# Rotating q and k out of PSUM, with the norm's factor moved behind the rotation

## The chip, the core and the metric

The kernel runs on one core of one Trainium2 chip. Its time is the device time of one execution in microseconds (us). A core has five engines that run beside each other, each through its own queue in order: TensorE (PE; its weight loads are listed as PEld), VectorE (DVE), ScalarE (ACT), GpSimd (POOL) and SyncE (SP), which here issues the loads. They wait for one another through semaphores. Matrix products land in PSUM, which has eight banks; all other tiles are in SBUF.

## What is computed

One layer of a hybrid encoder, 256 positions of width 2048, in float32. The input projection of the normalised x gives q, k, v and two halves of a gated convolution. q and k are normalised per head vector of 128, rotated and used in differential attention: four heads with two softmaxes each, of which the second is subtracted with a factor. The output projection and a gated feed-forward layer follow. The part around the change:

```python
xn = rms_norm(h, norm1_g[l])
proj = jnp.einsum('bsd,dn->bsn', xn, w_in[l].astype(xn.dtype))
...
q = apply_rope(rms_norm(q, q_norm_g[l]), cos, sin)
k = apply_rope(rms_norm(k, k_norm_g[l]), cos, sin)
...
s = jnp.einsum('bqhcd,bkhcd->bhcqk', q_blk, k).astype(jnp.float32) * scale
s = jnp.where(mask[None, None, None], s, -jnp.inf)
p = jax.nn.softmax(s, axis=-1)
w = p[:, :, 0] - lam * p[:, :, 1]
return jnp.einsum('bhqk,bkhe->bqhe', w.astype(v.dtype), v)
...
att = rms_norm(att, subln_g[l]) * (1.0 - lambda_init)
```

The rotation is linear, so a factor per position and head vector may be applied before it or behind it; for q it may also be applied to the scores.

## The kernel before

Every large product is made of reduced-precision passes: an operand is split into a rounded part `hi` and a rest `lo`, and three matmuls (hi by hi, lo by hi, hi by lo) take the place of one. The weights stream through in **chunks** of 256 rows by 512 columns. For each chunk SyncE loads `raw`, ScalarE casts it to `whi` (`round_chunk`, L324), VectorE subtracts to `wlo` (`split_chunk`, L333), and TensorE multiplies (`multiply`): a first half of eight matmuls with `whi` (L363, L364) and a second half of four with `wlo` (L369), for the two row halves m = 0 and 1 of the sequence, into two PSUM banks `acc`. `whi` and `wlo` have three buffers each, and both are queued two chunks ahead.

`run_chunks` walks the chunks in one order: four column blocks for the convolution, then blocks k, q, k, q, v, v (eight chunks each, the very first block nine), then the output projection and the feed-forward layer. Counted from 0, the first q block ends with chunk 48, the second k block with 56, the second q block with 64, the v blocks with 72 and 80.

All other work is written as generators that are started when a block is done. `resume` steps each of them once in the middle of a chunk's multiplication and once at its end, so a `yield` is half a chunk and `lag(n)` is n of them. What a generator queues at a step stands in its engine's queue at that place and is executed in that order. Between these steps `run_side` puts the taps of the convolution (L549, `y`) on VectorE as long as a credit of time lasts, from which other work is deducted by `spend`. `room(n, hold)` holds a generator back until n of the four auxiliary PSUM banks are free by the program's own count `held`.

The steps around the change: `qk_rows`, for a block of q or k and one m, squares the four head vectors out of PSUM (`square_sum`, L459, ScalarE), makes the factor `f` on GpSimd (`rsqrt_mean` and L647; the power is L222), scales into `qn` (L651, ScalarE), rotates (L658 to L661, VectorE), transposes (L666, TensorE) and copies into `qT` or `kT` (L667, ScalarE). `attend_scores`, for a head, makes the scores `ps_s` (L682), masks them, takes the maximum `nmx` (L692), the exponentials `pr` (L701), the combined weights `wt` (L712 to L715) and their transposes (L723 to L725). `attend_values` multiplies with v into `ps_o` (L749), squares that (L459), makes the factor `ro` on GpSimd, scales to `att` (L763), transposes to `ps_at` (L771) and splits into `mahi` and `malo` (or `ahi` and `alo`; `split_scaled`, L237 and L238).

Of the kernel before, what the change touches and what calls it, by code (L numbers as in the profile page):

```python
# [18 lines left out]
P = 128  # L19
# [44 lines left out]
RAW_BUFS = 5  # L64
AUX = 4

LAG = (3, 2, 6)
HL_BUFS = 3

KTILE_US = 1.30  # L70
# [56 lines left out]
def tile_block(  # L127
# [143 lines left out]
    def spend(us):  # L271
        credit[0] -= us
# [181 lines left out]
    xT = {}  # L454
    rstd1 = [const.tile([P, 1], F32, tag=f"rstd1_{m}", name=f"rstd1_{m}") for m in range(NM)]

    def square_sum(src, accum, **kw):
        junk = pre.tile([P, N], F32, tag="junk", name="junk", bufs=1)
        act.activation(junk[:, : src.shape[-1]], src, AF.Square, accum_out=accum, **kw)  # L459
# [178 lines left out]
    def qk_rows(key, b, m, ps):  # L638

        G = N // DH  # L640
        spend(1.65)
        ss = small.tile([P, G], F32, tag="ssq", name="ssq")
        for j in range(G):
            square_sum(ps[:, j * DH : (j + 1) * DH], ss[:, j : j + 1], scale=rstd1[m])
        f = small.tile([P, G], F32, tag="fq", name="fq")
        rsqrt_mean(f, ss, DH, EPS)
        pool.tensor_scalar(f, f, rstd1[m], 0.0, ALU.mult, ALU.add)  # L647
        yield from lag(LAG[0])
        qn = pre.tile([P, G, DH], F32, tag="va", name="qn")
        for j in range(G):  # L650
            act.activation(qn[:, j, :], ps[:, j * DH : (j + 1) * DH], AF.Copy, scale=f[:, j : j + 1])  # L651
# [4 lines left out]
        hd = DH // 2  # L656
        bc = lambda ap, n: ap.unsqueeze(1).to_broadcast([P, G, n])
        dve.tensor_tensor(t1, qn, bc(tab[:, 0, :], DH), ALU.mult)  # L658
        dve.tensor_tensor(t2[:, :, :hd], qn[:, :, hd:], bc(tab[:, 1, :hd], hd), ALU.mult)
        dve.tensor_tensor(t2[:, :, hd:], qn[:, :, :hd], bc(tab[:, 1, hd:], hd), ALU.mult)  # L660
        dve.tensor_tensor(t1, t1, t2, ALU.add)  # L661
# [8 lines left out]
    wTs = {}  # L670
    eps_s = small.tile([P, H, NM], F32, tag="eps_s", name="eps_s", bufs=1)

    def attend_scores(hd):
        scs = []
        yield
        yield from room(2, 2)
        for m in range(NM):
            L = (m + 1) * P
            sc = aux_ps.tile([P, 2, S], F32, tag="aux", name="ps_s")
            for c in range(2):  # L680
                g = 2 * hd + c
                pe.matmul(sc[:, c, :L], qkT["q"][:, g, m * P : (m + 1) * P], qkT["k"][:, g, :L],  # L682
                          start=True, stop=True)
            scs.append(sc)
        yield from lag(2)
        nmxs, prs, sms = [], [], []
        for m in range(NM):
            L = (m + 1) * P
            sc = scs[m]
            dve.memset(sc[:CHUNK, :, L - CHUNK : L], MASKED)  # L690
            nmx = small.tile([P, 2], F32, tag="nmx", name="nmx")
            dve.tensor_reduce(nmx, sc[:, :, :L], AX.X, ALU.max, negate=True)  # L692
            nmxs.append(nmx)
        spend(0.1)
        yield from lag(3)
        for m in range(NM):
            L = (m + 1) * P
            pr = pre.tile([P, 2, S], F32, tag="pr", name="pr", bufs=4)
            sm = small.tile([P, 2], F32, tag="sm", name="sm")
            for c in range(2):  # L700
                act.activation(pr[:, c, :L], scs[m][:, c, :L], AF.Exp, bias=nmxs[m][:, c : c + 1],  # L701
                               accum_out=sm[:, c : c + 1])
            prs.append(pr)
            sms.append(sm)
        held[0] -= 2
        yield from lag(2)
        wts = []
        for m in range(NM):
            L = (m + 1) * P
            r = small.tile([P, 1], F32, tag="r", name="r")  # L710
            c = small.tile([P, 1], F32, tag="a1", name="c")
            dve.reciprocal(r, sms[m][:, 1:2])  # L712
            dve.scalar_tensor_tensor(c, sms[m][:, 0:1], neg_lam, r, ALU.mult, ALU.mult)
            wt = pre.tile([P, S], F32, tag="wt", name="wt", bufs=4)
            dve.scalar_tensor_tensor(wt[:, :L], prs[m][:, 1, :L], c, prs[m][:, 0, :L], ALU.mult, ALU.add)  # L715
            pool.tensor_scalar(eps_s[:, hd, m : m + 1], sms[m][:, 0:1], sms[m][:, 0:1], E * EPS, ALU.mult, ALU.mult)
# [6 lines left out]
        pe.transpose(pt[:, 0, :], wts[0][:, :P], ident)  # L723
        pe.transpose(pt[:, 1, :], wts[1][:, :P], ident)
        pe.transpose(pt[:, 2, :], wts[1][:, P:], ident)  # L725
# [14 lines left out]
    def attend_values(hd):  # L740
        while hd not in wTs:
            yield
        wT = wTs.pop(hd)
        atts = []
        yield from room(1, 1)
        o = aux_ps.tile([P, NM, E], F32, tag="aux", name="ps_o")
        for m in range(NM):
            for k in range(m + 1):
                pe.matmul(o[:, m, :], wT[:, (0 if m == 0 else 1 + k), :], v_sb[k][:, hd * E : (hd + 1) * E],  # L749
                          start=k == 0, stop=k == m)  # L750
        yield
        ss = small.tile([P, NM], F32, tag="sso", name="sso")
        for m in range(NM):
            square_sum(o[:, m, :], ss[:, m : m + 1])
        r = small.tile([P, NM], F32, tag="ro", name="ro")
        t = small.tile([P, 8], F32, tag="rsq", name="rsq")
        pool.tensor_tensor(ss, ss, eps_s[:, hd, :], ALU.add)
        pool.tensor_scalar(t[:, :NM], ss, 1.0 / E, 0.0, ALU.mult, ALU.add)
        pool.tensor_tensor(r, t[:, :NM], neghalf[:, :NM], ALU.pow)
        yield from lag(2)  # L760
        for m in range(NM):
            at_ = pre.tile([P, E], F32, tag="att", name="att", bufs=4)
            act.activation(at_, o[:, m, :], AF.Copy, scale=r[:, m : m + 1])  # L763
            atts.append(at_)
        held[0] -= 1
        yield
        yield from room(1)
        pt = aux_ps.tile([P, 2, S], F32, tag="aux", name="ps_at")
        for e in range(2):
            for m in range(NM):  # L770
                pe.transpose(pt[:, e, m * P : (m + 1) * P], atts[m][:, e * P : (e + 1) * P], ident)  # L771
# [526 lines left out]
```

## Time and profile before

| | |
|---|---|
| runs | 1041.3 us median of 3 (1040.77 to 1041.76) |
| profiled execution | 1042.43 us, span 1040.7 us |
| granted TensorE clock | 1.0 in every slice |
| q, k and v blocks with the attention | about 95 to 250 us of the span |

A row of a timeline has the start in us from the span's start, the time taken, engine, line and operation, the tile written and those read, sizes and count, and in brackets the engine's idle time before it with what ended that. A row of a group has count, busy us, the mean ns of one, and the idle time before. Matmuls overlap, so their progress is read from start to start.

### The profile page before, as it was taken

To read this page: it belongs to the slowest core of one execution; us is meant where nothing else is said; L and a number is where in the kernel's file an instruction comes from. 1 tells how busy PE (TensorE), PEld (TensorE's weight loads), DVE (VectorE), ACT (ScalarE), POOL (GpSimd) and SP (SyncE) were. 2 spreads that over 40 slices of the span, in tenths; PEclk is the share of its full clock that TensorE was granted. 3 is DMA by queue.
4 is the path that set the end of the run, shared out by engine and by line. 5 is a ranking of instruction groups with operands and counts; after the bars stand their busy time and mean duration, and the time that the engine had idled before them with its cause. 6 is when DMAs were issued, how large, how long until landed. Compare 5 with 4: busy or idle time off the path is not lost.

```text
span 1040.7 us, 13006 instructions
## 1 busy us (share of the span) xinstructions
PE 1028.6 (99%) x4639; PEld 847.4 (81%) x4639; DVE 925.5 (89%) x1117; ACT 642.2 (62%) x796; POOL 115.4 (11%) x159
## 2 busy tenths in 40 slices
PE   8999999999999999999999999999999999999998
PEld 7888887877888788888888888888888888888786
DVE  7899889899775599999999898989999989889887
ACT  7554666656656565776665656666757556667452
POOL 0130123222000100000102011000001110000010
PEclk9999999999999999999999999999999999999999
DMA  9657644554546667987989899879798979797773
GB/s 336 225 182 277 221 165 150 174 167 137 180 152 230 187 236 242 275 258 223 264 238 261 286 234 278 258 238 265 222 272 246 282 217 294 232 259 230 215 222 101
DMA packets 115664, 237.59 MB, mean 228 GB/s; under 512 B 7696, under 2 KB 8848, under 8 KB 115344
## 3 DMA queue, kind: packets, MB, share of 16 engines
q1 hardware_dynamic: 104864, 203.71, 58.2%
q0 software_dynamic: 10592, 33.04, 16.4%
q8 instruction: 36, 0.59, 0.2%
q14 instruction: 28, 0.23, 0.1%
q10 hardware_dynamic: 144, 0.03, 0.0%
HBM read 204.24 MB, written 9.44 MB: 205 GB/s over the span
## 4 chain that ended last, share of the span: by engine, by line
PE 62%; DVE 1%; DMA 1%; issue 0%; ACT 0%; DVEq 0%
PE q L1058 11%; PE q L1052 11%; PE q L1053 11%; PE q L1033 9%; PE q L1031 9%; PE q L1032 9%; PE acc L369 1%; DMA wlo<-raw 1%; PE ps_a L856 1%; PE acc L364 1%; PE acc L363 1%; DVE wlo L333 0%; DVE wlt L1014 0%; DVE wt L1004 0%; ACT wh L1010 0%
## 5 line engine op out<-in xcount | busy, mean ns | idle before, releaser
L324 ACT CAST whi<-raw 128x1024 fp32r<-128x1024 f32 (+1 forms) x257 | 265.8, 1049 | 119.7 <-PE acc L364 60.1
L333 DVE TENSOR_TENSOR wlo<-raw,whi 128x1024 fp32r<-128x1024 f32 (+1 forms) x211 | 253.8, 1215 | 43.0 <-ACT whi L324 42.7
L1010 ACT CAST wh<-wt 128x2048 fp32r<-128x2048 f32 x60 | 114.9, 1915 | 109.2 <-DVE wt L1006 109.1
L1014 DVE TENSOR_TENSOR wlt<-wt,wh 128x2048 fp32r<-128x2048 f32 x60 | 137.4, 2290 | 19.5 <-ACT wh L1010 19.4
L363 PE MATMUL acc<-whi,xhi 128*128 128x512 f32 x320 | 126.4, 395 | 2.4 <-ACT whi L324 2.3
L1052 PE MATMUL q<-whi,chi 128*128 128x512 f32 x320 | 125.2, 391 | 0.0
L364 PE MATMUL acc<-whi,xlo 128*128 128x512 f32 x320 | 124.8, 390 | 0.0
L1053 PE MATMUL q<-whi,clo 128*128 128x512 f32 x320 | 124.6, 389 | 0.0
L1031 PE MATMUL q<-wh,fhi 128*128 128x512 f32 x280 | 109.8, 392 | 0.0
L1032 PE MATMUL q<-wh,flo 128*128 128x512 f32 x280 | 108.9, 389 | 0.0
L1013 DVE TENSOR_TENSOR wlb<-wb,wh 128x1536 fp32r<-128x1536 f32 x60 | 105.1, 1751 | 1.0 <-ACT wh L1007 1.0
L549 DVE SCALAR_TENSOR_TENSOR y<-upad,cw,y 128x256 f32<-128x256 f32 x240 | 101.9, 479 | 2.2 <-ACT y L542 2.2
L328 POOL DMA_DIRECT2D wlo<-raw x46 | 39.7, 863 | 507.6 <-ACT wlo L327 294.3
L369 PE MATMUL acc<-wlo,xhi 128*128 128x512 f32 x320 | 87.8, 396 | 2.0 <-DVE wlo L333 1.9
L1007 ACT CAST wh<-wb 128x1536 fp32r<-128x1536 f32 x60 | 88.5, 1474 | 0.4 <-DMA wb<-in_w_gate_dram 0.4
L1058 PE MATMUL q<-wlo,chi 128*128 128x512 f32 x320 | 85.7, 390 | 0.6 <-DMA wlo<-raw 0.6
L1052 PE MATMUL q<-whi,ahi 128*128 128x512 f32 x192 | 74.9, 390 | 0.0
L1053 PE MATMUL q<-whi,alo 128*128 128x512 f32 x192 | 74.7, 389 | 0.0
L1004 DVE TENSOR_TENSOR wt<-wb 128x1024 f32<-128x1024 f32 x60 | 73.0, 1217 | 0.0
L363 PEld LDWEIGHTS acc<-whi,xhi 128*128 128x128 f32 x320 | 60.1, 188 | 15.6 <-ACT whi L324 3.3
L369 PEld LDWEIGHTS acc<-wlo,xhi 128*128 128x128 f32 x320 | 59.3, 188 | 15.5 <-DVE wlo L333 3.6
L1058 PEld LDWEIGHTS q<-wlo,chi 128*128 128x128 f32 x320 | 59.9, 188 | 13.7 <-DMA wlo<-raw 1.2
(244 smaller groups left out, 1844.4 us busy)
## 6 DMA issues: line engine op xcount, KB each, us to landing
raw<-in_w_in_dram SPq DMA_DIRECT2D x79, 512.0 KB, 4.7
raw<-in_w_gate_dram SPq DMA_DIRECT2D x48, 512.0 KB, 5.4
raw<-in_w_up_dram SPq DMA_DIRECT2D x48, 512.0 KB, 5.2
raw<-in_w_down_dram SPq DMA_DIRECT2D x48, 512.0 KB, 7.1
wlo<-raw POOLq DMA_DIRECT2D x46, 512.0 KB, 7.3
wb<-in_w_up_dram SPq DMA_DIRECT2D x40, 512.0 KB, 4.5
wb<-in_w_gate_dram SPq DMA_DIRECT2D x40, 512.0 KB, 5.9
wb<-in_w_down_dram SPq DMA_DIRECT2D x40, 512.0 KB, 6.1
```

The costliest lines, as they stand in the source:

```text
L324: act.copy(c["hi"], c["raw"])
L333: dve.tensor_tensor(c["lo"], c["raw"], c["hi"].bitcast(F32), ALU.subtract)
L363: pe.matmul(ps[m], xhi[:, ms], hi[:, j, :], start=c["first"] and j == 0, stop=False)
L364: pe.matmul(ps[m], xlo[:, ms], hi[:, j, :], start=False, stop=False)
L369: pe.matmul(ps[m], xhi[:, ms], lo[:, j, :], start=False, stop=c["last"] and j == nk - 1)
L1010: act.copy(c["hi"][:, :SUMMED], c["t"])
L1014: dve.tensor_tensor(lot, c["t"], c["hi"][:, :SUMMED].bitcast(F32), ALU.subtract)
L1031: pe.matmul(ps, hi, c["hi"][:, w], start=bool(first), stop=False)
L1032: pe.matmul(ps, lo, c["hi"][:, w], start=False, stop=False)
L1052: pe.matmul(ps, xs[i][0][:, ms], hi[:, i, :], start=i == 0 and bool(c["first"].get(qs[m])), stop=False)
L1053: pe.matmul(ps, xs[i][1][:, ms], hi[:, i, :], start=False, stop=False)
L1058: pe.matmul(sum_bank(c, qs[m]), xs[i][0][:, ms], lo[:, i, :], start=False, stop=i == 1 and bool(c["last"].get(qs[m])))
```

## The change

`qk_rows` no longer makes `qn`. The squares are taken without the first norm's factor; the epsilon term that this factor brings in is made once for each m (`eps1`). The rotation reads the projection out of PSUM, with no factor. k's factor is applied by ScalarE behind the rotation, in place; q's factor goes into the exponential as its `scale`, and the maximum `nmx` is multiplied with it. The lags are shorter, and the copies out of the transposes are queued `COPY_LAG` half chunks later, with the PSUM bank held as long. In `attend_values` both halves are first rounded by ScalarE and then split by VectorE, and one GpSimd step is folded into the squares' scale.

```diff
-MASKED = -3.0e38
+MASKED = -1.0e30
...
-LAG = (3, 2, 6)
+LAG = (1, 3, 3)
+COPY_LAG = 2
...
+            pool.tensor_scalar(eps1[m], ss[:, m : m + 1], -2.0 * EPS / D, EPS * EPS, ALU.mult, ALU.add)
...
         for j in range(G):
-            square_sum(ps[:, j * DH : (j + 1) * DH], ss[:, j : j + 1], scale=rstd1[m])
-        f = small.tile([P, G], F32, tag="fq", name="fq")
-        rsqrt_mean(f, ss, DH, EPS)
-        pool.tensor_scalar(f, f, rstd1[m], 0.0, ALU.mult, ALU.add)
+            square_sum(ps[:, j * DH : (j + 1) * DH], ss[:, j : j + 1], scale=DH ** -0.5)
+        f = small.tile([P, G], F32, tag="f" + key, name="f" + key, bufs=4)
+        pool.tensor_scalar(ss, ss, eps1[m], 1.0, ALU.add, ALU.mult)
+        pool.tensor_tensor(f, ss, neghalf[:, :G], ALU.pow)
+        if key == "q":
+            fqs[b, m] = f
         yield from lag(LAG[0])
-        qn = pre.tile([P, G, DH], F32, tag="va", name="qn")
-        for j in range(G):
-            act.activation(qn[:, j, :], ps[:, j * DH : (j + 1) * DH], AF.Copy, scale=f[:, j : j + 1])
-        yield from lag(LAG[1])
...
-        dve.tensor_tensor(t1, qn, bc(tab[:, 0, :], DH), ALU.mult)
-        dve.tensor_tensor(t2[:, :, :hd], qn[:, :, hd:], bc(tab[:, 1, :hd], hd), ALU.mult)
-        dve.tensor_tensor(t2[:, :, hd:], qn[:, :, :hd], bc(tab[:, 1, hd:], hd), ALU.mult)
+        dve.tensor_tensor(t1, raw, bc(tab[:, 0, :], DH), ALU.mult)
+        dve.tensor_tensor(t2[:, :, :hd], raw[:, :, hd:], bc(tab[:, 1, :hd], hd), ALU.mult)
+        dve.tensor_tensor(t2[:, :, hd:], raw[:, :, :hd], bc(tab[:, 1, hd:], hd), ALU.mult)
         dve.tensor_tensor(t1, t1, t2, ALU.add)
-        yield from lag(LAG[2])
-        yield from room(1)
+        yield from lag(LAG[1])
+        if key == "k":
+            for j in range(G):
+                act.activation(t1[:, j, :], t1[:, j, :], AF.Copy, scale=f[:, j : j + 1])
+            yield from lag(LAG[2])
+        yield from room(1, 1)
         pt = aux_ps.tile([P, G, P], F32, tag="aux", name="ps_qk")
         for j in range(G):
             pe.transpose(pt[:, j, :], t1[:, j, :], ident)
+        yield from lag(COPY_LAG)
+        held[0] -= 1
         act.copy(qkT[key][:, b * G : (b + 1) * G, m * P : (m + 1) * P], pt)
...
+            f = fqs[hd // 2, m][:, hd % 2 * 2 : hd % 2 * 2 + 2]
+            dve.tensor_tensor(nmx, nmx, f, ALU.mult)
...
                 act.activation(pr[:, c, :L], scs[m][:, c, :L], AF.Exp, bias=nmxs[m][:, c : c + 1],
-                               accum_out=sm[:, c : c + 1])
+                               scale=fs[m][:, c : c + 1], accum_out=sm[:, c : c + 1])
...
-            split_scaled(mixa[2 * hd + e], pt[:, e, :], col("sg", e))
+            act.activation(mixa[2 * hd + e][0], pt[:, e, :], AF.Copy, scale=col("sg", e))
+        for e in range(2):
+            hi, lo = mixa[2 * hd + e]
+            dve.scalar_tensor_tensor(lo, pt[:, e, :], col("sg", e), hi.bitcast(F32), ALU.mult, ALU.subtract)
```

The instructions move. VectorE's queue at the first q block, before (`wlo` are those of chunks 52, 53 and 54; `t` is the rotated tile, `y` the taps of the convolution):

```order
L549 SCALAR_TENSOR_TENSOR y<-upad_127,cw,y 128x256 x2
L333 TENSOR_TENSOR wlo<-raw,whi 128x1024 x3
L658 TENSOR_TENSOR t_1515<-qn,gcsq_588 128x512
L659 TENSOR_TENSOR t_1516<-qn,gcsq_588 128x4x64
L660 TENSOR_TENSOR t_1516<-qn,gcsq_588 128x4x64
L661 TENSOR_TENSOR t_1515<-t_1515,t_1516 128x512
L549 SCALAR_TENSOR_TENSOR y<-upad_127,cw,y 128x256 x3
L333 TENSOR_TENSOR wlo<-raw,whi 128x1024
```

And with the change, at the same place, where the lines from L324 on are numbered one higher and the rotation is L661 to L664:

```order
L553 SCALAR_TENSOR_TENSOR y<-upad_129,cw,y 128x256 x2
L334 TENSOR_TENSOR wlo<-raw,whi 128x1024
L661 TENSOR_TENSOR t_1456<-acc,gcsq_592 128x512
L662 TENSOR_TENSOR t_1457<-acc,gcsq_592 128x4x64
L663 TENSOR_TENSOR t_1457<-acc,gcsq_592 128x4x64
L664 TENSOR_TENSOR t_1456<-t_1456,t_1457 128x512
L334 TENSOR_TENSOR wlo<-raw,whi 128x1024
L661 TENSOR_TENSOR t_1492<-acc,gcsq_596 128x512
L662 TENSOR_TENSOR t_1493<-acc,gcsq_596 128x4x64
L663 TENSOR_TENSOR t_1493<-acc,gcsq_596 128x4x64
L664 TENSOR_TENSOR t_1492<-t_1492,t_1493 128x512
L334 TENSOR_TENSOR wlo<-raw,whi 128x1024
```

The two rotations of a block stand two chunks earlier, one behind the `wlo` of chunk 52 and one behind that of 53, and read `acc`, the PSUM bank. TensorE's transposes of the rotated q move with them, from the ends of chunks 55 and 56 to the middles of 52 and 53.

ScalarE's queue behind the v copies, where head 0's output is squared (`junk,sso`), before; `att` is head 0's, then head 1's, and `pr` the exponentials of head 2, the only ones there:

```order
L734 ACTIVATE v_134<-acc,rstd_1_123 128x512
L324 CAST whi<-raw 128x1024 x2
L459 ACTIVATE junk,sso<-ps_o 128x256 x4
L324 CAST whi<-raw 128x1024
L763 ACTIVATE att<-ps_o,ro 128x256 x2
L701 ACTIVATE pr,sm<-ps_s,nmx 128x128 x2
L701 ACTIVATE pr,sm<-ps_s,nmx 128x256 x2
L237 ACTIVATE mahi<-ps_at,cols 128x256 x2
L763 ACTIVATE att<-ps_o,ro 128x256 x2
```

With the change, at the same place (`pr` is first head 2's, then head 3's):

```order
L747 ACTIVATE v_136<-acc,rstd_1_123 128x512
L325 CAST whi<-raw 128x1024
L714 ACTIVATE pr,sm<-ps_s,nmx,fq 128x128 x2
L714 ACTIVATE pr,sm<-ps_s,nmx,fq 128x256 x2
L325 CAST whi<-raw 128x1024
L462 ACTIVATE junk,sso<-ps_o 128x256 x4
L325 CAST whi<-raw 128x1024
L714 ACTIVATE pr,sm<-ps_s,nmx,fq 128x128 x2
L714 ACTIVATE pr,sm<-ps_s,nmx,fq 128x256 x2
L774 ACTIVATE att<-ps_o,ro 128x256 x2
L786 ACTIVATE mahi<-ps_at,cols 128x256 x2
L774 ACTIVATE att<-ps_o,ro 128x256 x2
```

The exponentials of head 3 have come up from behind head 1's split to a place ahead of head 0's `att`.

More of the change, by code (lines that the diff above doesn't have):

```diff
@@ L455, in tile_block @@
     rstd1 = [const.tile([P, 1], F32, tag=f"rstd1_{m}", name=f"rstd1_{m}") for m in range(NM)]
+    eps1 = [const.tile([P, 1], F32, tag=f"eps1_{m}", name=f"eps1_{m}") for m in range(NM)]
     def square_sum(src, accum, **kw):
@@ L656, in qk_rows @@
         hd = DH // 2
+        raw = ps.rearrange("p (g d) -> p g d", g=G)
         bc = lambda ap, n: ap.unsqueeze(1).to_broadcast([P, G, n])
-        dve.tensor_tensor(t1, qn, bc(tab[:, 0, :], DH), ALU.mult)
-        dve.tensor_tensor(t2[:, :, :hd], qn[:, :, hd:], bc(tab[:, 1, :hd], hd), ALU.mult)
-        dve.tensor_tensor(t2[:, :, hd:], qn[:, :, :hd], bc(tab[:, 1, hd:], hd), ALU.mult)
+        dve.tensor_tensor(t1, raw, bc(tab[:, 0, :], DH), ALU.mult)
+        dve.tensor_tensor(t2[:, :, :hd], raw[:, :, hd:], bc(tab[:, 1, :hd], hd), ALU.mult)
+        dve.tensor_tensor(t2[:, :, hd:], raw[:, :, :hd], bc(tab[:, 1, hd:], hd), ALU.mult)
         dve.tensor_tensor(t1, t1, t2, ALU.add)
-        yield from lag(LAG[2])
-        yield from room(1)
+        yield from lag(LAG[1])
[4 more added lines that the diff above has]
+        yield from room(1, 1)
         pt = aux_ps.tile([P, G, P], F32, tag="aux", name="ps_qk")
@@ L670, in tile_block @@
     wTs = {}
+    fqs = {}
     eps_s = small.tile([P, H, NM], F32, tag="eps_s", name="eps_s", bufs=1)
@@ L685, in attend_scores @@
         yield from lag(2)
-        nmxs, prs, sms = [], [], []
+        nmxs, fs, prs, sms = [], [], [], []
         for m in range(NM):
@@ L692, in attend_scores @@
             dve.tensor_reduce(nmx, sc[:, :, :L], AX.X, ALU.max, negate=True)
+            f = fqs[hd // 2, m][:, hd % 2 * 2 : hd % 2 * 2 + 2]
+            dve.tensor_tensor(nmx, nmx, f, ALU.mult)
             nmxs.append(nmx)
+            fs.append(f)
         spend(0.1)
@@ L753, in attend_values @@
         for m in range(NM):
-            square_sum(o[:, m, :], ss[:, m : m + 1])
+            square_sum(o[:, m, :], ss[:, m : m + 1], scale=E ** -0.5)
         r = small.tile([P, NM], F32, tag="ro", name="ro")
-        t = small.tile([P, 8], F32, tag="rsq", name="rsq")
         pool.tensor_tensor(ss, ss, eps_s[:, hd, :], ALU.add)
-        pool.tensor_scalar(t[:, :NM], ss, 1.0 / E, 0.0, ALU.mult, ALU.add)
-        pool.tensor_tensor(r, t[:, :NM], neghalf[:, :NM], ALU.pow)
+        pool.tensor_tensor(r, ss, neghalf[:, :NM], ALU.pow)
         yield from lag(2)
```

2 lines of the change are left out of this document (1 added, 1 removed).

## The prediction

> **What bounds the kernel now.** I read the page's busy times first: TensorE is busy for nearly the whole span.
>
> ```profile
> PE 1028.6 (99%) x4639; PEld 847.4 (81%) x4639; DVE 925.5 (89%) x1117; ACT 642.2 (62%) x796; POOL 115.4 (11%) x159
> ```
>
> So an edit on the other engines is worth only the time in which TensorE stands still. Then the windows, here two of 25 us in the stage of the change (the span, then busy time and count of PE, PEld, DVE, ACT and POOL): TensorE misses 0.80 and 1.14 us in them.
>
> ```profile
> 150.00:175.00 25.00, 24.20 (x113) 19.77 (x113) 21.55 (x38) 16.61 (x40) 6.66 (x10) 1.00 0.43 138
> 200.00:225.00 25.00, 23.86 (x113) 19.57 (x111) 22.65 (x41) 13.96 (x28) 4.83 (x5) 1.00 0.49 161
> ```
>
> TensorE's timeline shows each place. Starts follow each other every 0.23 us (163.42 to 163.65); what a start comes later than that is lost.
>
> ```profile
> 163.42 0.39 PE L363 MATMUL acc<-whi,xhi 128*128 128x512 f32 x1
> 163.65 0.39 PE L364 MATMUL acc<-whi,xlo 128*128 128x512 f32 x1
> 164.83 1.21 PE L369 MATMUL acc<-wlo,xhi 128*128 128x512 f32 x4 [0.80 <-DVE wlo L333]
> 190.50 0.39 PE L364 MATMUL acc<-whi,xlo 128*128 128x512 f32 x1
> 190.98 0.73 PE L369 MATMUL acc<-wlo,xhi 128*128 128x512 f32 x2
> 213.99 0.39 PE L364 MATMUL acc<-whi,xlo 128*128 128x512 f32 x1
> 215.52 0.97 PE L369 MATMUL acc<-wlo,xhi 128*128 128x512 f32 x3 [1.14 <-DVE wlo L333]
> 250.05 0.39 PE L364 MATMUL acc<-whi,malo 128*128 128x512 f32 x1
> 250.55 0.30 PE L723 MATMUL ps_wt<-ident,wt 128*128 128x128 f32 x1
> 251.31 0.33 PE L724 MATMUL ps_wt<-ident,wt 128*128 128x128 f32 x1 [0.46 <-DVE wt L715]
> 251.47 0.27 PE L725 MATMUL ps_wt<-ident,wt 128*128 128x128 f32 x1
> 262.67 0.39 PE L364 MATMUL acc<-whi,malo 128*128 128x512 f32 x1
> 263.43 0.67 PE L771 MATMUL ps_at<-ident,att 128*128 128x128 f32 x4 [0.37 <-DVE alo L238]
> ```
>
> Three times a second half waits for `wlo`: 1.18 - 0.23 = 0.95, 0.48 - 0.23 = 0.25 and 1.53 - 0.23 = 1.30 us, together **2.50**. The weights of head 3 come late: 0.50 - 0.23 = 0.27, and 0.76 less the 0.16 from one transpose to the next, 0.60, together **0.87**. The last transposes of `att` come late by 0.76 - 0.23 = **0.53**. In all 3.90 us, the most that better order can give here.
>
> Why is `wlo` late? VectorE's, ScalarE's and GpSimd's timelines around the first q block:
>
> ```profile
> 148.78 2.35 DVE L333 TENSOR_TENSOR wlo<-raw,whi 128x1024 fp32r<-128x1024 f32 x2
> 154.51 1.22 DVE L333 TENSOR_TENSOR wlo<-raw,whi 128x1024 fp32r<-128x1024 f32 x1 [3.38 <-ACT whi L324]
> 155.65 0.69 DVE L658 TENSOR_TENSOR t<-qn,gcsq 128x512 f32<-128x512 f32 x1
> 157.04 0.69 DVE L661 TENSOR_TENSOR t<-t,t 128x512 f32<-128x512 f32 x1
> 157.65 1.27 DVE L549 SCALAR_TENSOR_TENSOR y<-upad,cw,y 128x256 f32<-128x256 f32 x3
> 148.59 3.40 POOL L222 TENSOR_TENSOR fq<-rsq,neghalf 128x4 f32<-128x4 f32 x1
> 147.80 0.19 ACT L459 ACTIVATION_READ_ACCUMULATOR junk<-acc,rstd 128x1 f32 x1
> 150.58 0.19 ACT L459 ACTIVATION_READ_ACCUMULATOR junk<-acc,rstd 128x1 f32 x1
> 152.40 1.14 ACT L651 ACTIVATE qn<-acc,fq 128x128 f32<-128x128 f32 x4 [1.62 <-POOL fq L647]
> 153.41 1.07 ACT L324 CAST whi<-raw 128x1024 fp32r<-128x1024 f32 x1
> 205.60 1.23 DVE L333 TENSOR_TENSOR wlo<-raw,whi 128x1024 fp32r<-128x1024 f32 x1 [2.28 <-ACT whi L324]
> ```
>
> ScalarE stands before `qn` until GpSimd's power is done; the cast `whi` is queued behind that, and VectorE idles 3.38 us for it. Then VectorE has two rotations to make up and falls behind. At the second q block it idles 2.28 us in the same way, before the wait at 215.52.
>
> **The change part by part.** *The scaling between squares and rotation goes.* ScalarE loses 32 `qn` (four take 1.14 us above, so 9 us) and has 16 of the same form behind k's rotation, off the path both. VectorE's rotation keeps its time if a read of PSUM costs what a read of SBUF does.
>
> ```profile
> L788 DVE TENSOR_TENSOR h<-h,acc 128x512 f32<-128x512 f32 x8 | 5.1, 680 | 0.0
> L713 DVE SCALAR_TENSOR_TENSOR c<-sm,neg_lam,r 128x1 f32<-128x1 f32 x8 | 1.8, 220 | 0.4
> ```
>
> An add of that size with one operand in PSUM takes 680 ns, the rotation's own, wholly in SBUF, 0.69 us (157.04): I take no difference. [...]
>
> Now walk VectorE's queue in its new order (its rows stand in the section on the change) from where it stood, 148.78, though it should be earlier, since k's copies no longer hold ScalarE. One `wlo` is 1.13 to the next start (half of 148.78's pair), a rotation 157.65 - 155.65 = 2.00. First rotation 149.91 to 151.91: the squares that it must follow ended at 147.99. `wlo`, then second rotation 153.04 to 155.04; its squares ended at 150.77. Third `wlo` from 155.04, done 1.22 later at 156.26. TensorE's second halves stood there:
>
> ```profile
> 152.53 1.07 PE L369 MATMUL acc<-wlo,xhi 128*128 128x512 f32 x4
> 157.97 1.07 PE L369 MATMUL acc<-wlo,xhi 128*128 128x512 f32 x4
> ```
>
> The one at 157.97 takes that `wlo`, so it is 1.7 us early, and VectorE never idles. The 0.95 goes; the second q block has the same pattern (2.28 idle), so the 1.30 goes. The 0.25 lies in the k block, where softmax and rotation came on one another's heels; they stand apart now. All 2.50 is taken as gained. On the other side of that bound stands zero, if `wlo` is late for another reason.
>
> *Added on VectorE:* eight tiny products on `nmx`, by the nearest row 0.22 us each, 1.8 us over some 60 us; the windows show VectorE idle over 2 us in each 25. Nothing on the path, and 0.2 us each if that cover were gone. *Exponentials with a second pointer operand:* ScalarE's rows with none, one and two pointers (L459, L763, L611) differ by 87 and 88 ns.
>
> ```profile
> L459 ACT ACTIVATE junk<-ps_o 128x256 f32<-128x256 f32 x8 | 3.1, 385 | 7.9 <-PE ps_o L749 7.7
> L763 ACT ACTIVATE att<-ps_o,ro 128x256 f32<-128x256 f32 x8 | 3.3, 472 | 0.0
> L611 ACT ACTIVATE z<-ps_ln,cols 128x256 f32<-128x256 f32 x8 | 4.2, 560 | 1.2 <-DVE mclo L615 1.1
> ```
>
> *Transposes and scores move two or three chunks ahead*; TensorE does the same number, so nothing for itself. *Copies queued later* end ScalarE's waits for transposes, which were beside the path. *The two halves of the split of `att`* no longer take turns: `att` of head 3 is some 0.6 us earlier, which covers the 0.53. Head 3's weights are transposed in the middle of chunk 79 in place of 82; VectorE makes them right behind that chunk's `wlo`, and no longer runs behind there, so I take the 0.87 as gained. If VectorE is as late there as at 250.55, it stays.
>
> *A new wait.* Head 3's four exponentials now stand ahead of head 0's `att` (ScalarE's rows in the section on the change). Before:
>
> ```profile
> 231.94 0.60 PE L771 MATMUL ps_at<-ident,att 128*128 128x128 f32 x4
> 230.33 0.84 ACT L763 ACTIVATE att<-ps_o,ro 128x256 f32<-128x256 f32 x2
> 231.06 0.37 ACT L701 ACTIVATE pr<-ps_s,nmx 128x128 f32<-128x128 f32 x1
> 232.64 0.51 ACT L237 ACTIVATE mahi<-ps_at,cols 128x256 fp32r<-128x256 f32 x1
> 262.67 0.83 ACT L763 ACTIVATE att<-ps_o,ro 128x256 f32<-128x256 f32 x2
> ```
>
> ScalarE's place there is tied to TensorE (it squares `ps_o` as soon as that is made), so it doesn't come earlier. The exponentials take 232.64 - 231.06 = 1.58, with the second pointer 1.58 + 4 x 0.09 = 1.94. `att` starts at 230.33 + 1.94 = 232.27, and from its start to the transposes are 263.43 - 262.67 = 0.76: 233.03, against 231.94. New loss **1.1 us**; 0.7 if the pointer hides in the overlap, none if the order leaves ScalarE ahead. Behind it wait `mahi`, head 1's `att` and its transposes, half a chunk later.
>
> Sum: 3.90 - 1.1 = **2.8 us** gained. The profiled execution took 1042.43 (span 1040.7), so 1039.6; that execution was 1.1 above the median of the runs, 1041.3, and so I forecast 1038.5.
>
> **The rivals.** *No new wait* at head 0: 3.9 gained, 1037.4. For it: exponentials may be done before the squares are. Against: they are queued behind them.
>
> *TensorE reaches the rotated q too early.* The transposes now follow the rotation by 1.5 chunks. In the walk the first rotation's last row ends at 149.91 + 1.39 + 0.69 = 151.99, TensorE arrives at 152.53: only 0.54 early. Where VectorE is 0.9 later than walked, each q block loses some 0.5: 1.0 off the gain, 1039.5. [...]
>
> *The waits stay*, because `wlo` is late by VectorE's load and not by its idling: 0.87 + 0.53 - 1.1 = 0.3 gained, 1041.0. Against it: the 3.38 and 2.28 idle.
>
> *Slower: the rotation waits for ScalarE.* Both read one PSUM bank, and in the order of the new kernel the rotation waits for the squares, with every `wlo` behind it. If that wait is as long as the old 3.38, a q block loses 3.38 - 0.54 = 2.8 at its transposes and a k block 3.38 - 1.7 = 1.7 at its `wlo`: 2 x 2.8 + 2 x 1.7 = 9.0 against 2.8, 1047.5. It decides from a wait w with 2 (w - 0.54) = 2.8, w = 1.9. Against: the squares ended 1.9 and 2.3 us before their turns in the walk. For: in the second k block exponentials stand ahead of the squares. [...]
>
> [...]
>
> **How the numbers follow.** Forecast 0.52, no new wait 0.10, transposes too early 0.15, waits stay 0.11, slower 0.12. The 0.2% that a measurement can tell here is 2.1 us, 1039.2 to 1043.4. The first two are faster: 0.62; the next two within: 0.26; the last slower: 0.12. The range goes from all 3.9 with a little more (each wait also costs the matmul behind it), 1037.0, to past the case that the waits stay, 1041.8; it leaves out the slower case.
>
> **What would show it.** Right: no `wlo` wait of TensorE between 150 and 250, VectorE not idle for `whi` at the q blocks, three reading operations of about 680, 420 and 420 ns, and a wait of about 1 us for `att` near 230. Wrong: TensorE waiting for `t1` before the q transposes, VectorE idle before the rotation with ScalarE's squares as releaser, or a rotation longer than 2.2 us.

## The result, and the profile after

The changed kernel takes 1038.48 us (median of 8 runs, 1038.03 to 1039.06), the kernel before 1041.46 (8 runs beside them, 1040.77 to 1042.19): ratio 0.9972, 95% interval 0.9963 to 0.9981, 3.0 us. The forecast was 1038.5. The profiled execution took 1038.44, span 1036.7.

The busy times hardly moved, TensorE's by 0.3 us:

```profile
PE 1028.9 (99%) x4639; PEld 848.7 (82%) x4639; DVE 926.5 (89%) x1125; ACT 638.3 (62%) x780; POOL 110.8 (11%) x149
```

So the 3 us were waits. What TensorE still waits for in the whole execution (the waits by line: total us, times, longest):

```profile
PE ps_warm L162 <- POOL neghalf L156: 1.4, 1, 1.4
PE acc L364 <- ACT whi L325: 0.9, 2, 0.5
PE ps_at L782 <- ACT att L774: 0.8, 1, 0.8
...
```

No `wlo`, no `ps_wt`, and for `att` one wait, the forecast one. The first two rows lie in the first 10 us; what is left out are two waits of 0.3 and 0.2 us behind 350. The windows (span; busy of PE, PEld, DVE, ACT, POOL) show the same: TensorE is busy throughout at the first q block, where it had missed 0.80 us (and at the second, where it had missed 1.14), and misses 0.80 us in the window of the new wait.

```profile
150.00:175.00 25.00, 25.00 (x119) 20.84 (x118) 24.45 (x49) 14.91 (x35) 4.58 (x8) 1.00 0.57 190
...
225.00:250.00 25.00, 24.20 (x114) 19.70 (x113) 20.61 (x45) 15.97 (x32) 2.69 (x5) 1.00 0.38 126
```

VectorE's timeline at the first q block, with the end of ScalarE's squares of the two row blocks (L462) and TensorE's transposes of the first (L673):

```profile
146.70 1.22 DVE L334 TENSOR_TENSOR wlo<-raw,whi 128x1024 fp32r<-128x1024 f32 x1
147.84 0.68 DVE L661 TENSOR_TENSOR t<-acc,gcsq 128x512 f32<-128x512 f32 x1
149.22 0.69 DVE L664 TENSOR_TENSOR t<-t,t 128x512 f32<-128x512 f32 x1
149.83 1.22 DVE L334 TENSOR_TENSOR wlo<-raw,whi 128x1024 fp32r<-128x1024 f32 x1
150.96 0.68 DVE L661 TENSOR_TENSOR t<-acc,gcsq 128x512 f32<-128x512 f32 x1
152.95 1.22 DVE L334 TENSOR_TENSOR wlo<-raw,whi 128x1024 fp32r<-128x1024 f32 x1
146.64 0.19 ACT L462 ACTIVATION_READ_ACCUMULATOR junk<-acc 128x1 f32 x1
149.36 0.19 ACT L462 ACTIVATION_READ_ACCUMULATOR junk<-acc 128x1 f32 x1
152.29 0.60 PE L673 MATMUL ps_qk<-ident,t 128*128 128x128 f32 x4
```

No idle stands in these rows where 3.38 us did. The order is the forecast one, 2.08 us sooner than walked (146.70 for 148.78). One idle of VectorE for `whi` is left ahead of them, 1.52 us at 143.18, where ScalarE has waited for the convolution's `ps_y`; TensorE doesn't wait for it.

Executions begin up to 1.2 us apart, since the loads that ScalarE's first casts wait for come at different times (idle of 0 to 2.22 us before a cast). Cleaner than the span is a stretch between two rows of TensorE, from the group of second halves at 14.99 (14.61 after) to the read-out `ps_r` at 358.48 (354.91), behind all that the change touches (that group starts between 14.21 and 15.43 in the runs below).

```profile
14.99 1.07 PE L369 MATMUL acc<-wlo,xhi 128*128 128x512 f32 x4
358.48 0.62 PE L943 MATMUL ps_r<-ident,rep 128*128 128x128 f32 x2 [0.33 <-ACT rep L939]
```

```profile
14.61 1.07 PE L370 MATMUL acc<-wlo,xhi 128*128 128x512 f32 x4
354.91 0.62 PE L957 MATMUL ps_r<-ident,rep 128*128 128x128 f32 x2 [0.32 <-ACT rep L953]
```

343.49 us before, 340.30 after: **3.19 us** gained in the stretch. A second trace of the kernel before gives 343.42, so it repeats to 0.1 us, and single waits can be told apart in it that the run times cannot. All experiments are read by it:

| run | median us | ratio to before, 95% | stretch against before, us |
|---|---|---|---|
| before, again | 1041.27 (one run) | | -0.07 |
| changed kernel | 1038.48 | 0.9972 (0.9963 to 0.9981) | -3.19 |
| e1 exponentials behind `att` | 1038.33 | 0.9969 (0.9958 to 0.9981) | -3.51 |
| e2 before, scale later | 1038.48 | 0.9974 (0.9963 to 0.9985) | -2.87 |
| e3 before, credit with the work | 1038.67 | 0.9976 (0.9967 to 0.9984) | -2.86 |
| e4 rotation late | 1040.16 | 0.9989 (0.9980 to 0.9998) | -1.95 |
| e5 copies at once | 1037.86 | 0.9963 (0.9950 to 0.9975) | -3.92 |
| e6 split in turn | 1039.47 | 0.9979 (0.9970 to 0.9988) | -2.32 |
| e7 before, power twice | 1045.94 | 1.0039 (1.0027 to 1.0052) | +4.13 |
| e8 e1, weights sooner | 1037.13 | 0.9961 (0.9948 to 0.9973) | -4.43 |
| e9 squares twice | 1039.34 | 0.9982 (0.9973 to 0.9991) | -2.60 |
| e10 before, two orders | 1037.87 | 0.9968 (0.9956 to 0.9980) | -4.32 |

### The profile page after: what moved, and what is told of

It is laid out like the page before. It is cut to its first block, busy times and chain, and to the rows that moved or that the text cites. A ratio compares the mean times of both kernels' runs of the same rounds, so it can differ in the third digit from the quotient of the medians.

```text
span 1036.7 us, 13003 instructions
## 1 busy us (share of the span) xinstructions
PE 1028.9 (99%) x4639; PEld 848.7 (82%) x4639; DVE 926.5 (89%) x1125; ACT 638.3 (62%) x780; POOL 110.8 (11%) x149
## 4 chain that ended last, share of the span: by engine, by line
PE 63%; DVE 2%; issue 1%; ACT 0%; DVEq 0%
PE q L1066 11%; PE q L1067 11%; PE q L1072 11%; PE q L1047 9%; PE q L1045 9%; PE q L1046 9%; PE ps_a L870 1%; PE acc L370 1%; PE acc L364 1%; PE acc L365 1%; DVE wlo L334 1%; DVE wlt L1028 0%; DVE wt L1018 0%; DVE wt L1019 0%; ACT wh L1024 0%
## 5 line engine op out<-in xcount | busy, mean ns | idle before, releaser
L365 PEld LDWEIGHTS acc<-whi,xlo 128*128 128x128 f32 x320 | 60.4, 189 | 12.6
```

Source lines behind the costliest of these rows:

```text
L365: pe.matmul(ps[m], xlo[:, ms], hi[:, j, :], start=False, stop=False)
```

## The experiments

Theory 1 is the prediction's: the gain is VectorE's idle, which came through the cast `whi` that stood behind a ScalarE waiting for GpSimd's power. Against it stand: (2) the place, the rotation's credit being taken two chunks before its work lands; (3) VectorE's load; (4) the copies queued later.

**e2, the cause taken away by ScalarE's order alone.** The kernel before, with

```
-LAG = (3, 2, 6)
+LAG = (4, 1, 6)
```

> The kernel before with the scaling qn queued half a chunk later, behind the next cast whi; TensorE's and VectorE's queues are word for word those of before, only ScalarE's order differs, and the rotation still reads qn from SBUF. Theory 1 (wlo was late because whi stood behind a ScalarE that waited for GpSimd's power): VectorE's idle of 3.38 and 2.28 us at the two q blocks falls below 1.2 us each, the waits of 0.95 and 1.30 go, the ones at head 3's weights and at att stay; about 2.2 us gained on before: 1039.2, ratio 0.998. Rival 2 (the place: the credit for the rotation is taken from VectorE's filler work two chunks before the rotation lands, so VectorE runs out of work there whoever holds whi): the idle and the waits stay, 1041.4. Rival 3 (VectorE's load): the same 1041.4, with the idle gone and the waits there.

Theory 1 held, and by more than expected: 1038.48, stretch -2.87, as much as the whole change by the run times, with the rotation still reading `qn` in SBUF. VectorE's queue, word for word that of before, now reads at the first q block (its idle, then what ScalarE waits for):

```profile
151.12 1.22 DVE L333 TENSOR_TENSOR wlo<-raw,whi 128x1024 fp32r<-128x1024 f32 x1 [0.63 <-ACT whi L324]
153.69 0.69 DVE L658 TENSOR_TENSOR t<-qn,gcsq 128x512 f32<-128x512 f32 x1 [1.35 <-ACT qn L651]
152.51 1.15 ACT L651 ACTIVATE qn<-acc,fq 128x128 f32<-128x128 f32 x4 [1.43 <-POOL fq L647]
```

ScalarE still waits 1.43 us for GpSimd, but `whi` is no longer behind that wait. VectorE's idle is 1.98 in two pieces, the larger behind the third `wlo`, and so above the 1.2 expected; a further 1.19 us stands ahead of these rows, at 144.62. At the second q block none is left. So at the first block about as much idle is left as before, but in three short pieces, and TensorE waits for none of them. All three `wlo` waits are gone, the 0.25 too.

**e7, a double dose of the cause.** The kernel before, with

```
         f = small.tile([P, G], F32, tag="fq", name="fq")
+        pool.tensor_scalar(f, ss, 1.0 / DH, EPS, ALU.mult, ALU.add)
+        pool.tensor_tensor(f, f, neghalf[:, :G], ALU.pow)
         rsqrt_mean(f, ss, DH, EPS)
```

> The kernel before with GpSimd's scaling and power for the rotation's factor made twice in a row (the first result isn't used): a dose more of the suspected cost, on an engine that is busy 11% of the span. Theory 1: ScalarE waits for GpSimd by 1.2 us more (298 + 1,010 ns as the undisturbed rows have them) or more where VectorE's next wlo falls beside it, VectorE's idle at the two q blocks grows from 3.38 and 2.28 by about as much, the waits of TensorE for wlo by 1 to 1.5 us each, and the k block between gets one: 2 to 4 us slower than before, 1043.5 to 1045.5, ratio 1.002 to 1.004. Rivals 2 and 3 (place, load): 1041.4.

4.3 us slower (1045.94 against 1041.60 beside it), stretch +4.13: a little over the upper end of theory 1, and nothing that (2) or (3) allow. ScalarE's scaling waits for GpSimd 15.8 us in all (4.8 before; the groups), and VectorE's idle is 3.67 at both q blocks. Only part of the loss is where it was expected. The 0.25 at the k block between became 1.22 (193.24). But TensorE's waits for `wlo` at the q blocks did not grow by 1 us each (0.95 and 0.68 in the profile, for 0.80 and 1.14); in their place it waits for `whi` itself, 0.68, 0.37 and 0.99:

```profile
L653 ACT ACTIVATE qn<-acc,fq 128x128 f32<-128x128 f32 x32 | 9.2, 369 | 15.8 <-POOL fq L649 15.8
```

```profile
155.28 1.23 DVE L333 TENSOR_TENSOR wlo<-raw,whi 128x1024 fp32r<-128x1024 f32 x1 [3.67 <-ACT whi L324]
193.24 1.19 PE L369 MATMUL acc<-wlo,xhi 128*128 128x512 f32 x4 [1.22 <-DVE wlo L333]
213.29 0.50 PE L363 MATMUL acc<-whi,xhi 128*128 128x512 f32 x1 [0.99 <-ACT whi L324]
```

At the first q block the idle grew by only 0.29 us: the 3.40 us power of before is here 1.01 us twice, since another operation of GpSimd met VectorE's two `wlo`: the scaling between the two powers, 0.19 us elsewhere, took 2.59 (last section). What grew is the time until the second scaling (ScalarE waits 1.95 us more ahead of it), with the next `whi` behind it.

**e3, the idle filled in place of removed.** The kernel before, with the credit moved:

```
-        spend(1.65)
         ss = small.tile([P, G], F32, tag="ssq", name="ssq")
...
         yield from lag(LAG[1])
+        spend(1.65)
```

> The kernel before with the 1.65 us of the rotation taken from the filler's credit where the rotation is queued, not where the squares are; ScalarE still waits for GpSimd. VectorE has three or four conv taps (1.2 to 1.6 us) more between two wlo where it idled, and as many fewer behind the rotations. Theory 1 with idle as the cost: the taps fill 2.5 of the 3.38 us, VectorE is not behind afterwards, the waits of 0.95 and 1.30 go or fall below 0.3 each: 1039.0 to 1040.0. Rival 3 (waits stay since VectorE is simply overloaded there): 1041.4. Rival 2 (the place of the credit) expects the full 2.25 here, and nothing in the kernel whose scale is queued later.

1038.67, stretch -2.86: the waits are gone, with the same load on VectorE, so (3) falls. The gain is above what theory 1 expected here (1039.0 to 1040.0); by its size alone this run speaks for (2). VectorE idles 1.01 us where it idled 3.38 (0.99 at the second block).

```profile
153.53 1.23 DVE L333 TENSOR_TENSOR wlo<-raw,whi 128x1024 fp32r<-128x1024 f32 x1 [1.01 <-ACT whi L324]
148.35 1.13 POOL L222 TENSOR_TENSOR fq<-rsq,neghalf 128x4 f32<-128x4 f32 x1
```

This run and e2 reach the same by two ways, so the place of the credit (2) is real too: taps at that place keep VectorE at work while `whi` is late. As the only cause (2) is out: it had the idle and the waits stay in e2, and they went.

**e4, the rotation from PSUM at its old place.** The changed kernel with

```
-LAG = (1, 3, 3)
+LAG = (5, 3, 3)
```

> The changed kernel, but with the rotation queued two chunks later as in the kernel before: it reads PSUM, needs no factor, and ScalarE doesn't wait for GpSimd, but the credit is taken two chunks before the rotation lands and three wlo stand in a row on VectorE. Theory 1: whi is not held, VectorE idles under 1.2 us at the q blocks, no wlo wait of TensorE over 0.3 us between 150 and 250 us: the changed kernel's time within 0.5 (1038.0 to 1039.0). Rival 2 (the place): VectorE idles 2 us or more there, one wait of about 1 us for wlo at each q block comes back: 1040.5 to 1041.0.

Neither: 1040.16, stretch -1.95, and TensorE's losses are elsewhere than either theory said. At the q blocks there is no `wlo` wait (VectorE's idle at the first is 1.36, above theory 1's 1.2 and below the 2 of (2), and none at the second). But everything behind q comes two chunks later, and softmax then meets head 0's output:

```profile
228.38 0.71 PE L692 MATMUL ps_s<-kT,qT 128*128 128x128 f32 x4 [0.21 <-ACT pr L714]
229.47 1.13 PE L692 MATMUL ps_s<-kT,qT 128*128 128x256 f32 x4 [0.38 <-ACT pr L714]
232.88 0.88 DVE L789 SCALAR_TENSOR_TENSOR malo<-ps_at,cols,mahi 128x256 fp32r<-128x256 f32 x2 [3.78 <-ACT mahi L786]
243.53 1.20 PE L370 MATMUL acc<-wlo,xhi 128*128 128x512 f32 x4 [0.70 <-DVE wlo L334]
```

Scores wait until exponentials give their PSUM buffers back, VectorE idles 3.78 us for `mahi`, and a `wlo` is late 11 us behind that, in place of the changed kernel's one wait at `att`. So the earlier rotation is worth 1.2 us here, by what follows it, not by its own place.

**e1, the new wait taken away.** The changed kernel with head 3's exponentials two half-chunks later:

```
-        yield from lag(3)
+        yield from lag(5 if hd == 3 else 3)
```

> The changed kernel with head 3's exponentials queued two half-chunks later, behind att of heads 0 and 1; nothing else differs. My theory of the new wait (TensorE at 231.18 waits 0.93 + 0.14 us because head 3's four exponentials stand ahead of att on ScalarE): both excesses go, the transposes of att at that place start within 0.1 us of the matmul before, and about 1.0 us is gained on the changed kernel (some 1037.4 us, ratio to before 0.996). Rival (att waits for VectorE, GpSimd or ps_o at that place, whatever stands ahead of it): a wait of 0.8 us or more stays and the time is the changed kernel's. A danger for both: the weights of head 3 are made later, and their transposes, half a chunk later too, could wait as they did in the kernel before (0.87).

The wait went, so its cause is shown. TensorE and ScalarE there in the changed kernel:

```profile
229.35 1.07 PE L370 MATMUL acc<-wlo,xhi 128*128 128x512 f32 x4
231.18 0.91 PE L782 MATMUL ps_at<-ident,att 128*128 128x128 f32 x4 [0.77 <-ACT att L774]
228.68 0.46 ACT L714 ACTIVATE pr<-ps_s,nmx,fq 128x128 f32<-128x128 f32 x1
230.64 0.85 ACT L774 ACTIVATE att<-ps_o,ro 128x256 f32<-128x256 f32 x2
```

The transposes come 231.18 - 229.35 - 4 x 0.23 = 0.91 us late and take 0.91 in place of 0.60: 1.2 us in all. In e1 they start at 230.23 and take 0.60. But the danger named came as well: head 3's weights are late, and only 0.32 us of the stretch is gained.

```profile
230.23 0.60 PE L782 MATMUL ps_at<-ident,att 128*128 128x128 f32 x4
241.76 0.30 PE L736 MATMUL ps_wt<-ident,wt 128*128 128x128 f32 x1
242.51 0.33 PE L737 MATMUL ps_wt<-ident,wt 128*128 128x128 f32 x1 [0.46 <-DVE wt L728]
```

**e8, both waits taken away.** e1, and

```
-        yield from lag(2)        # between exponentials and weights
+        yield from lag(1 if hd == 3 else 2)
...
-        yield from lag(4)        # between weights and their transposes
+        yield from lag(5 if hd == 3 else 4)
```

> The changed kernel with head 3's exponentials behind att of heads 0 and 1, as in the run that took the new wait away and brought back 0.76 us at head 3's weights; now VectorE's queue makes the weights a half-chunk sooner after the exponentials (ahead of a wlo and four taps that stood before them), and TensorE's queue is unchanged. If those two waits are all that is left: weights done 2 us sooner, no wait over 0.2 us between 120 and 350 us, 0.76 us gained on that run, 1.06 on the changed kernel: 1037.5, ratio 0.996. Rival (the weights wait for ScalarE's exponentials, not for VectorE's queue): the 0.76 stays.

1037.13, the lowest median of all; in the stretch 4.43 us under the kernel before and 1.24 under the changed kernel. No wait of TensorE is left between 15 and 350 us; the weights' transposes start 0.11 apart:

```profile
241.24 0.27 PE L736 MATMUL ps_wt<-ident,wt 128*128 128x128 f32 x1
241.35 0.27 PE L737 MATMUL ps_wt<-ident,wt 128*128 128x128 f32 x1
```

**e5, the copies queued at once.** The changed kernel with

```
-COPY_LAG = 2
+COPY_LAG = 0
```

> The changed kernel with the copies of the rotated q and k queued right behind their transposes again, as before; the rest of the change stays. Theory 1 (the gain is VectorE's idle, through the cast behind ScalarE's wait for GpSimd): the copies were beside the path, so no wait for wlo at the q blocks and the changed kernel's time within 0.6 us: 1038.0 to 1039.1. Rival 4 (the later copies are what lets ScalarE cast in time): ScalarE waits for transposes 5 us or more in all again (7.6 and 11.9 before, 0.6 and 0.0 in the changed kernel), whi is late by it, and at least 1 us of the gain goes: 1039.5 or more.

(4) has the wrong sign: 1037.86, a little under theory 1's range, stretch -3.92, 0.73 better without the later copies. ScalarE does wait for the transposes again (groups: 4.4 and 7.6 us; changed kernel 0.6 and 0.0), beside the path:

```profile
L676 ACT COPY qT<-ps_qk 128x512 f32<-128x512 f32 x4 | 2.4, 588 | 7.6 <-PE ps_qk L673 7.6
L676 ACT COPY kT<-ps_qk 128x512 f32<-128x512 f32 x4 | 2.3, 584 | 4.4 <-PE ps_qk L673 4.4
```

The gain is at `att`: scores, which wait for the last copy, come up to two half-chunks earlier, the exponentials of head 3 with them, and of the new wait's 0.91 us before the first transpose 0.27 is left by the same reckoning (230.67 - 229.48 - 4 x 0.23), though the transposes still take 0.91. So the later copies, which take waits from ScalarE, are what pushed the exponentials ahead of `att`.

**e6, the split in turn.** The changed kernel with the two halves taking turns again:

```
-            act.activation(mixa[2 * hd + e][0], pt[:, e, :], AF.Copy, scale=col("sg", e))
-        for e in range(2):
-            hi, lo = mixa[2 * hd + e]
-            dve.scalar_tensor_tensor(lo, pt[:, e, :], col("sg", e), hi.bitcast(F32), ALU.mult, ALU.subtract)
+            split_scaled(mixa[2 * hd + e], pt[:, e, :], col("sg", e))
```

> The changed kernel with ScalarE and VectorE taking turns on the two halves of the split of att again. As I worked it out, the 0.53 at the last transposes of att comes back, and nothing else: 0.5 us more than the changed kernel, 1039.0, seen in the trace more than in the time. Rival (the earlier att comes from elsewhere, as from heads 2 and 3 moved ahead): the wait there stays away, and the time is the changed kernel's. VectorE's one idle of 2.56 us for mahi at head 0 parts into two, of 2.5 and 0.5.

The wait at the last transposes of `att` returns, as expected; the price is 0.87 of the stretch, not 0.5. The starts of the same matmuls in both traces put about 0.3 of it at head 1's transposes (0.85 us in place of 0.60), whose `att` now stands behind a `mahi` that waits for `malo`, and 0.54 here:

```profile
260.70 0.67 PE L782 MATMUL ps_at<-ident,att 128*128 128x128 f32 x4 [0.35 <-DVE alo L239]
```

**e9, a dose of the slower rival.** The changed kernel with every square made twice:

```
+        s2 = small.tile([P, G], F32, tag="ssq2", name="ssq2")
+        for t in (s2, ss):
             for j in range(G):
-                square_sum(ps[...], ss[:, j : j + 1], scale=DH ** -0.5)
+                square_sum(ps[...], t[:, j : j + 1], scale=DH ** -0.5)
```

> The changed kernel with ScalarE's four squares of each row block made twice in a row (the first sums aren't used), 4 x 0.48 us more on ScalarE ahead of each rotation: a dose of the slower rival, in which the rotation waits for ScalarE's squares. In the changed kernel the squares of the first q block ended 1.0 and 1.5 us before the rotations began. If the wait is real: VectorE idles 0.7 to 1.5 us before the first reading operation of a rotation, with the squares as releaser, in the q blocks and the first k block. What it costs: TensorE reached the q transposes 2 us and more behind the rotation's end, so at most one wait of some 0.5 us, mostly for wlo or t in the second k block: 1038.5 to 1040.0. If the rival's price were right (2.8 us from each q block once the wait is 1.9 or more), 1041 or more. If the rotation doesn't wait, no idle with that releaser, 1038.5.

The rival's wait is real: VectorE idles before the rotation with the squares as releaser.

```profile
148.05 0.69 DVE L663 TENSOR_TENSOR t<-acc,gcsq 128x512 f32<-128x512 f32 x1 [0.50 <-ACT junk L462]
152.05 0.69 DVE L663 TENSOR_TENSOR t<-acc,gcsq 128x512 f32<-128x512 f32 x1 [0.79 <-ACT junk L462]
```

At these sizes, short of the 1.9 us from which the rival was to decide, it costs nothing at the q blocks; 0.59 us of the stretch goes, nearly all of it at the second k block, where TensorE reaches four transposes at 181.38 while ScalarE, behind exponentials, is still scaling the rotated k: they take 1.20 us in place of 0.60. The changed kernel stands 1.0 and 1.4 us clear of this wait, and beyond that has 2.4 us more before TensorE arrives.

**e10, only orders.** The kernel before with e2's `LAG` and the split of `att` in two halves as the change has it (e6's minus lines for its plus line).

> The kernel before with two changes of order alone: the scaling qn half a chunk later on ScalarE (as in the run that had the scale later), and the split of att made of both first halves, then both second halves. No rotation from PSUM, no second pointer, copies at once. If the three wlo waits (2.9 us with what follows them) and the 0.53 at att are all that the change as a whole gained but for head 3's weights (0.87), which then stay, against the changed kernel's new wait (1.06), which this kernel doesn't have: 3.4 us gained on before, 1038.0, at or just under the changed kernel's. Rival: a part of the gain needs the rotation out of PSUM: 1039.0 or more.

1037.87, stretch -4.32: without rotation from PSUM, second pointer or later copies, two changes of order do more than the whole change. Of the 0.9 more than expected, the starts of the same matmuls in e2 and here put 0.6 at head 3's weights: in e2 TensorE's wait there is 0.46, here 0.15, and the first of them is no longer late. Ahead of them VectorE idles 1.46 us for `mahi` here and 2.17 in e2. Another 0.2 came at second halves that were a little late in the kernel before (244.69) and that neither the prediction nor the expectation had counted.

**e11, the kernel before again.**

> The kernel before, unchanged, for a second trace of it. The order of each engine is fixed, so the waits for wlo at the two q blocks and the k block (0.95, 0.25, 1.30), those at head 3's weights (0.27 and 0.53) and at att (0.53), and VectorE's idle of 3.38 and 2.28 us, return within 0.1 us. The one wait of the first trace that no edit of this change can reach (0.75 us, for a wlo some 70 us before the end) is smaller or gone if it comes from the transfers of one execution.

Every wait and idle returned within 0.05 us, as these two did:

```profile
215.25 1.20 PE L369 MATMUL acc<-wlo,xhi 128*128 128x512 f32 x4 [1.15 <-DVE wlo L333]
154.24 1.23 DVE L333 TENSOR_TENSOR wlo<-raw,whi 128x1024 fp32r<-128x1024 f32 x1 [3.38 <-ACT whi L324]
```

What did not return is a wait for a transfer in the first trace, which explains most of why that execution was 1.1 us above the median:

```profile
971.15 1.20 PE L1058 MATMUL q<-wlo,chi 128*128 128x512 f32 x4 [0.59 <-DMA wlo<-raw]
```

## Why the prediction was right, step by step

- **The three `wlo` waits, 2.50: right in place and cause, too small in size.** e2 removes just these, and the stretch gains 2.87. The difference is behind each wait: the four second halves that follow take 1.21 us in the prediction's row at 164.83 and 1.07 in the undisturbed ones, 0.14 more. The prediction gave this to the range ("each wait also costs the matmul behind it"); it belonged in the sum, 0.12 for each wait. For the 0.25 the reason was wrong: e2 removes it with softmax and rotation where they were, so it too came through ScalarE's order. And the length of an idle is not its price: the kernel before has one of 2.57 us at the first k block (128.62), which cost TensorE nothing. Nor is all of the 3.38 GpSimd's: from 151.13, where the pair of `wlo` ends, ScalarE waits for it until 152.40, some 1.3 us; the rest is the scaling and the cast itself.
- **Head 3's weights, 0.87: gained, with more reason than given.** The new place suffices, as said (e6 has it without the halves, and no wait there); but e10 shows that the halves of the split alone take most of the waiting away at the old place too, because VectorE idles less for `mahi`. The prediction counted the halves at `att` only.
- **`att`, 0.53: right.** e6 brings back 0.54 there, and about 0.3 more at head 1's transposes that the prediction hadn't seen.
- **The new wait, 1.1: right, 1.2 measured,** and e8, without it, gains 1.24 in the stretch. The exponentials take 230.64 - 228.68 = 1.96 (1.94 taken). From the start of `att` to the transposes are 0.54, not 0.76; the slower transposes behind the wait make up for it.
- **The sum, 2.8:** with these sizes 2.87 + 0.87 + 0.53 - 1.22 = 3.05; the stretch shows 3.19, the run times 3.0. That the time came out within 0.02 us of the forecast is luck: the gain was 0.2 to 0.4 us larger, and the kernel before measured 1041.46 beside it and not 1041.3. The 3.90 called the most that order can give was too low: e8 gains 4.43 and e10 4.32.
- **A PSUM read costs what an SBUF read does: right here.** The rotation's first operation from PSUM and from SBUF, after and before:

```profile
L661 DVE TENSOR_TENSOR t<-acc,gcsq 128x512 f32<-128x512 f32 x4 | 2.7, 684 | 0.0
L704 DVE TENSOR_TENSOR nmx<-nmx,fq 128x2 f32<-128x2 f32 x8 | 1.3, 161 | 0.9 <-DVE nmx L702 0.5
L714 ACT ACTIVATE pr<-ps_s,nmx,fq 128x128 f32<-128x128 f32 x8 | 3.6, 450 | 0.0
```

```profile
L658 DVE TENSOR_TENSOR t<-qn,gcsq 128x512 f32<-128x512 f32 x4 | 2.7, 685 | 0.0
L701 ACT ACTIVATE pr<-ps_s,nmx 128x128 f32<-128x128 f32 x8 | 2.9, 374 | 3.0 <-DVE nmx L692 3.0
```

684 against 685 ns, and the two half-size reads take 414 and 415 ns against 419 and 418: "no difference", taken from two rows of before, held. The second pointer costs 76 ns in the row, 0.09 from start to start as taken; the products on `nmx` 161 ns, not 220, and off the path.
- **VectorE's walk from 148.78: 2.1 us too late,** as the prediction allowed. So the rival "TensorE reaches the rotated q too early", at 0.54 us of margin, was far: the first rotation ends at 149.22 + 0.69 = 149.91, and TensorE comes at 152.29, 2.4 us behind.
- **The slower rival:** its wait exists (e9), but its price was reckoned with 0.54 us to spare before the transposes, and there are 2.4. At waits of 0.50 and 0.79 us the q blocks paid nothing; no run made the wait as long as 1.9. The kernel before already had a wait between two readers of one PSUM tile: ScalarE's second `mahi` and VectorE's first `malo` both read `ps_at`, and `mahi` stood 0.55 us until `malo` was done. That the shared bank is the cause, there or at the rotation, was not shown.

```profile
233.69 0.47 ACT L237 ACTIVATE mahi<-ps_at,cols 128x256 fp32r<-128x256 f32 x1 [0.55 <-DVE malo L238]
```

- **"Copies queued later end ScalarE's waits, which were beside the path": right, and not the whole of it.** Their cost, 0.73 us, was already in the new wait, whose cause I had put on the order without saying that the later copies make it.

## What to carry to other kernels

An engine that waits for a slow neighbour holds whatever stands behind it in its queue (here ScalarE waited 1.62 us for GpSimd, and VectorE idled 3.38 for the cast behind that): look there before making the neighbour's work go away, since moving the waiting step behind the next step that others need (e2) gave nearly the same as the rewriting that did away with it (2.87 and 3.19 us of the stretch). When waits are removed one at a time, the next thing in the same queue shows up (e1, e4); follow the chain to the end before judging an edit. For gains of a few tenths of a per cent, compare a stretch between two rows of the bound engine, not spans.

## What the runs showed of the hardware that was not expected

**Single small operations of GpSimd took about 2.4 us longer here, as long as VectorE's pair of `wlo` beside them.** The prediction took GpSimd's 3.40 us power as its price. It is 1.01 us at the second row block (152.72), and the rest fits VectorE: two `wlo` of 2.35 us together ran at that time. At the second q block the power took 1.13 and the tiny scaling behind it, 0.27 elsewhere, met the pair: 2.62 = 0.27 + 2.35. GpSimd in the kernel before, the first row at the first q block:

```profile
148.59 3.40 POOL L222 TENSOR_TENSOR fq<-rsq,neghalf 128x4 f32<-128x4 f32 x1
200.83 2.62 POOL L647 TENSOR_SCALAR fq<-fq,rstd 128x4 f32<-128x4 f32 x1
204.93 0.27 POOL L647 TENSOR_SCALAR fq<-fq,rstd 128x4 f32<-128x4 f32 x1
124.58 1.02 POOL L222 TENSOR_TENSOR fq<-rsq,neghalf 128x4 f32<-128x4 f32 x1
```

Not every overlap does this. In the last row a power began while VectorE stood idle; a `wlo` followed 0.24 us later (124.82), and neither was held. The first two began while VectorE still had a tap under way, with the two `wlo` right behind it.

So the old wait at the q blocks was in part a ring: VectorE's `wlo` held GpSimd (2.39 of the 3.40 us), GpSimd held ScalarE (1.62), ScalarE held `whi`, and VectorE idled 3.38 us for `whi`. No run changes `wlo` alone, so this is read from the rows and not shown by an experiment. With the change the power runs beside a rotation that reads PSUM, and takes 1.01 us:

```profile
148.14 1.01 POOL L651 TENSOR_TENSOR fq<-ssq,neghalf 128x4 f32<-128x4 f32 x1
```

The taps of the convolution beside it (e3, 148.35) lengthen it by 0.12 only. In e7 it is the scaling between the two powers, 0.19 us undisturbed, that meets the pair: 2.59 us at the first q block and 2.57 at the second, beside pairs of 2.37 and 2.35. The `wlo` at 124.82 took its usual 1.23 us beside a power that had begun first. What makes GpSimd's operation longer, and why the taps lengthen it so little, no run here shows.
